# Layer 0's values, gates and reciprocal sums kept in DRAM by block of 128 tokens

## The chip, the cores and the metric

The kernel runs on one core of a Trainium2 chip. The metric is the device time of one execution, in microseconds (us). A core has five engines that work side by side: TensorE (PE; matmuls, its weight loads are listed as PEld), VectorE (DVE), ScalarE (ACT), GpSimd (POOL) and SyncE (SP). SP computes nothing: it issues DMA transfers from an in-order queue, and when one transfer has to wait, all behind it in that queue wait too.

## The reference, cut to what matters

A two-layer decoder on x of 2048 tokens by 1024 features, all in float32. Layer 0 runs two attentions of 8 heads each over one input projection, multiplies their joined output by a SiLU gate, projects it, and adds and normalises. Layer 1 (sliding window) does the same with other heads and is not touched by the change.

```
h = x @ w_in
cq, ckv, k_pe, fq, fk, fv, f_logit, gate = _split(h, EVEN_SIZES)
...
o_mla = causal_block_attention(q_mla, k_mla, v_mla, (MLA_NOPE + MLA_ROPE) ** -0.5)
...
o_fox = causal_block_attention(_heads(fq, FOX_HEADS), _heads(fk, FOX_HEADS),
                               _heads(fv, FOX_HEADS), FOX_DIM ** -0.5, cum)
o = jnp.concatenate([_merge(o_mla), _merge(o_fox)], axis=-1)
return (o * jax.nn.silu(gate)) @ w_out
```

and then `x = layer_norm(ALPHA * x + y, g, b)`.

## The kernel before

Five phases follow each other. Phase 1 (to about 595 us of the span) projects x; among its results are the SiLU gates, which `feature_tile` stores to the DRAM tensor `g1`, 32 stores of 256 KB. Phase 2 (to about 1522 us) runs the 16 heads of layer 0, each in four chunks `c` of 512 query tokens. `produce` makes the unnormalised probabilities of one chunk and stores the reciprocals of their row sums to `rd`; `consume` turns them and multiplies by the values, and stores the unnormalised output to `og1[c]` (64 stores of 128 KB). The two run interleaved: while one chunk is produced, the one before it is consumed. Phase 3 is the output projection of layer 0: 16 blocks `t` of 128 tokens. `load_og` loads a block's gates (`load_gate`, tile gt), the reciprocal sums (two loads, each spread over 64 partitions, tile rb) and values (tile og), multiplies them on POOL and DVE, and splits the product into a high part `oh` (ACT) and a low part `ol` (DVE); `out_block` then runs 48 matmuls of 128x512 (eight weight tiles, three products each, two halves), adds x, takes the statistics, and every second block normalises two blocks and stores them to `x1` (`finish`). Phases 4 and 5 are layer 1.

What sets the order around the change: a scheduler arranges the instructions of each engine, and each engine then runs its list in order. Nearly all loads of phases 2 and 3 share SP's queue. In phase 3 the gates and sums of a block are loaded into the buffers that later hold its `oh` and `ol` (three of each), so they wait until an earlier block's matmuls have freed them. The values have one buffer:

```
og = opool.tile([128, KB, 128], F32, name="og", bufs=1)
```

so the values of the next block are issued only when `ol` of the block before has been made from it. The rows z of x have five buffers, and a z load waits for the store of a block five earlier. Two blocks are prepared ahead by `prefetch`, which runs during the last chunk of the last head: it loads output weights, the gates and values of tokens 0 to 255, and multiplies them on POOL.

Of the kernel before, what the change touches and what calls it, by code (L numbers as in the profile page):

```python
# [9 lines left out]
F32 = mybir.dt.float32  # L10
# [29 lines left out]
def decoder_trunk(ctx, tc, x, x_t, w_lat, w_main, w_u, g_lat, b_f, w_out1, ln1,  # L40
# [20 lines left out]
    rd = dram.tile([16, T], F32, name="rd")  # L61
    g1 = dram.tile([D, T], F32, name="g1")
    og1 = [dram.tile([128, KB, 512], F32, name=f"og1_{c}") for c in range(4)]
# [122 lines left out]
    def phase1(late):  # L186
# [145 lines left out]
        def feature_tile(n, m, chunk, xT, w):  # L332
# [14 lines left out]
            else:  # L347
# [4 lines left out]
                queue.dma_start(out=g1[p * 128:(p + 1) * 128, tcs], in_=sg[:])  # L352
# [124 lines left out]
    def load_gate(gt, rb, t0, n):  # L477

        nc.sync.dma_start(out=gt, in_=g1[:, t0:t0 + n].rearrange("(k p) t -> p k t", p=128))
        for s_ in range(2):  # L480
            nc.sync.dma_start(out=rb[s_ * 64:s_ * 64 + 64], in_=rd[:].rearrange("(k s) t -> s k t", s=2)[s_:s_ + 1, :, t0:t0 + n].broadcast_to([64, KB, n]))

    def phase2(ctx, kpool):
# [25 lines left out]
        def produce(n, c, st):  # L509
# [55 lines left out]
            nc.sync.dma_start(out=rd[h if mla else 8 + h, tcs].rearrange("(j p) -> p j", p=128), in_=rec[:])  # L565

        def consume(n, c, P):
# [18 lines left out]
            def finish(po):  # L586
# [4 lines left out]
                queue.dma_start(out=og1[c][(hd % 2) * 64:(hd % 2) * 64 + 64, hd // 2, :], in_=t2[:])  # L591
# [45 lines left out]

        def prefetch():
# [9 lines left out]
            gts, rbs = (ppool.tile([128, T], F32, name="p")[:].rearrange("p (k q) -> p k q", k=KB) for _ in range(2))  # L648
            load_gate(gts, rbs, 0, 256)
            for t in range(2):  # L650
                nc.sync.dma_start(out=wout["og"][t], in_=og1[0][:, :, tok(t)])
            nc.gpsimd.tensor_tensor(out=gts, in0=gts, in1=rbs, op=OP.mult)
            for t in range(2):
                nc.gpsimd.tensor_tensor(out=wout["og"][t], in0=wout["og"][t], in1=gts[:, :, tok(t)], op=OP.mult)
            for steps, k, tag in ((PRE[0], 7, "vv"), (PRE[1], 4, "ka"), (PRE[2], 6, "kb")):
                for _ in range(steps):
                    yield 1
                wo_split(k, tag, raw[k], True)
            for _ in range(99):
                yield 1  # L660
# [6 lines left out]
        for n, c in todo + [(None, None)]:  # L667
            st = []
            gens = []
            if (n, c) == (15, 3):  # L670
                r3, r5 = wo_load(kpool.tile([128, T], F32, name="cb"), 3, 5)
            if n is None:
# [105 lines left out]
    def phase3(stack4, kpool, wout):  # L778
        with ExitStack() as ctx:
# [14 lines left out]
            def load_og(t):  # L794
                hl = parts()
                gt, rb = (bits(v[:]) for v in hl)
                load_gate(gt, rb, t * 128, 128)
                og = opool.tile([128, KB, 128], F32, name="og", bufs=1)
                nc.sync.dma_start(out=og[:], in_=og1[t // 4][:, :, tok(t % 4)])
# [462 lines left out]
```

## Time and profile before

| | us |
|---|---|
| median of 3 runs | 2666.89 (2655.42 to 2667.24) |
| the profiled execution, its own time | 2674.29 |
| its span, first to last instruction | 2672.5 |
| PE busy in the span | 2471.1 (92%) |
| mean granted TensorE clock | 0.962 |
| moved by DMA | 360.91 MB, 135 GB/s over the span |

The span is what the profile's rows are timed in; 1.8 us of the execution lie outside it. The profiled execution was 7.4 us slower than the median of the runs, so a saving read from its rows is taken off the median.

### The profile page before, as it was taken

The numbers are of one execution on the slowest core, as the hardware profiler recorded it, in microseconds if no ns is written. First come the engines' busy times: TensorE is split into PE (matmuls) and PEld (weight loads), VectorE is DVE, ScalarE is ACT, GpSimd is POOL, SyncE is SP. The second block draws the span as 40 slices with busy tenths as digits, with TensorE's granted clock in tenths as the row PEclk, the third lists the DMA queues.
The fourth block names the chain that finished last, engine by engine and source line by source line (L and its number), as shares of the span: only waits on it lengthen the run. The fifth ranks groups of instructions, "written<-read, shape, count | busy, mean of one in ns | idle before, by whom it ended". The sixth has DMA issues, their size and how long they took to land.

```text
span 2672.5 us, 36349 instructions
## 1 busy us (share of the span) xinstructions
PE 2471.1 (92%) x12885; PEld 2050.3 (77%) x12885; DVE 1531.1 (57%) x3002; ACT 1172.7 (44%) x2409; POOL 707.0 (26%) x694
## 2 busy tenths in 40 slices
PE   8999999999999999999999787659999999999997
PEld 7898888987788887888877665437888887777775
DVE  5442264317787877777777643345633644777775
ACT  3121222217676866777676501011121115566663
POOL 2010011101222221222222333232321321356555
PEclk9999999999999999999999888879999999999998
DMA  6574346654556665454554558854444653566563
GB/s 204 177 251 143 106 152 235 202 167 62 95 93 93 83 114 86 83 111 79 97 84 83 115 151 170 151 129 156 142 138 141 177 154 100 150 150 165 155 155 103
DMA packets 298566, 360.91 MB, mean 135 GB/s; under 512 B 55920, under 2 KB 202352, under 8 KB 293776
## 3 DMA queue, kind: packets, MB, share of 16 engines
q1 hardware_dynamic: 294224, 343.51, 53.6%
q0 software_dynamic: 4160, 15.08, 1.5%
q8 instruction: 102, 1.67, 0.3%
q14 instruction: 80, 0.66, 0.2%
HBM read 240.20 MB, written 118.29 MB: 134 GB/s over the span
## 4 chain that ended last, share of the span: by engine, by line
PE 68%; DMA 17%; DVE 5%; POOL 3%; ACT 3%; issue 3%; SPq 1%; POOLq 0%; DVEq 0%; ACTq 0%
PE pm L91 11%; PE pm L89 11%; PE pm L90 10%; PE pt L604 6%; DMA og<-og 5%; PE S L547 4%; PE S L548 4%; PE po L581 3%; PE po L582 3%; DMA kb<-kf 3%; DMA q<-qr 3%; DMA q<-qf 2%; PE S L1061 2%; PE py L727 2%; PE S L550 2%
## 5 line engine op out<-in xcount | busy, mean ns | idle before, releaser
L76 DVE TENSOR_TENSOR tl<-pt,th 128x512 fp32r<-128x512 f32 (+3 forms) x672 | 400.7, 611 | 128.4 <-ACT th L75 125.2
L89 PE MATMUL pm<-xh,w 128*128 128x512 f32 x1088 | 428.7, 394 | 7.5 <-DVE z L734 5.6
L75 ACT CAST th<-pt 128x512 fp32r<-128x512 f32 (+3 forms) x672 | 340.4, 524 | 203.2 <-PE pt L604 168.1
L91 PE MATMUL pm<-xh,w 128*128 128x512 f32 x1088 | 425.9, 392 | 0.0
L90 PE MATMUL pm<-xl,w 128*128 128x512 f32 x1088 | 425.6, 391 | 0.0
L604 PE MATMUL pt<-ident,p 128*128 128x128 f32 x2176 | 348.0, 280 | 4.0 <-DVE tl L76 3.9
L561 ACT ACTIVATE p<-p,mx 128x128 f32<-128x128 f32 (+15 forms) x256 | 309.0, 1207 | 29.3 <-DVE mx L558 27.5
L604 PEld LDWEIGHTS pt<-ident,p 128*128 128x128 f32 x2176 | 271.8, 145 | 58.6 <-DVE tl L76 7.3
L547 PE MATMUL S<-ka,q 96*128 96x512 f32 (+5 forms) x640 | 253.4, 396 | 29.6 <-DMA q<-qf 11.5
L581 PE MATMUL po<-th,vv 128*128 128x512 f32 (+2 forms) x640 | 278.0, 434 | 0.6 <-DVE t L589 0.4
L82 POOL TENSOR_SCALAR w<-w_raw 128x1024 fp32r<-128x1024 f32 (+3 forms) x88 | 98.5, 1132 | 581.3 <-PE pm L91 418.8
L89 PEld LDWEIGHTS pm<-xh,w 128*128 128x128 f32 x1088 | 205.0, 188 | 49.5 <-issue 7.3
L582 PE MATMUL po<-tl,vv 128*128 128x512 f32 (+2 forms) x640 | 238.3, 373 | 0.0
L91 PEld LDWEIGHTS pm<-xh,w 128*128 128x128 f32 x1088 | 204.7, 188 | 42.9
L90 PEld LDWEIGHTS pm<-xl,w 128*128 128x128 f32 x1088 | 204.9, 188 | 41.6
L609 POOL TENSOR_SCALAR th<-tf 128x512 fp32r<-128x512 f32 x96 | 59.4, 618 | 668.8 <-ACT tf L608 363.8
L548 PE MATMUL S<-kb,q 96*128 96x512 f32 (+5 forms) x640 | 234.4, 369 | 0.0
L83 DVE TENSOR_TENSOR w<-w_raw,w 128x1024 fp32r<-128x1024 f32 (+3 forms) x89 | 138.6, 1572 | 130.4 <-POOL w L82 127.4
L558 DVE CUSTOM_DVE_ANT_0 p<-S,zm 128x1024 f32<-128x1024 f32 (+7 forms) x128 | 123.7, 967 | 104.4 <-PE S L550 103.4
L547 PEld LDWEIGHTS S<-ka,q 128*128 128x128 f32 (+1 forms) x640 | 124.5, 194 | 54.5 <-issue 23.3
L1062 DVE CUSTOM_DVE_ANT_0 p<-S,bm,nsk 128x256 f32<-128x256 f32 x256 | 117.7, 477 | 71.8 <-PE S L1061 69.7
L1064 ACT ACTIVATE p<-p,mx 128x256 f32<-128x256 f32 x256 | 129.0, 505 | 66.2 <-DVE mx L1062 65.7
(249 smaller groups left out, 4771.0 us busy)
## 6 DMA issues: line engine op xcount, KB each, us to landing
w_raw<-in_w_main_dram SPq DMA_DIRECT2D x40, 512.0 KB, 5.2
w_raw<-in_w_odd_dram SPq DMA_DIRECT2D x36, 512.0 KB, 4.5
vd<-s_v SPq DMA_DIRECT2D x64, 256.0 KB, 2.7
vv<-vd SPq DMA_DIRECT2D x16, 1024.0 KB, 10.6
qs<-hl SPq DMA_DIRECT2D x64, 256.0 KB, 3.5
qt<-qs SPq DMA_DIRECT2D x64, 256.0 KB, 5.3
ka<-kf SPq DMA_DIRECT2D x16, 512.0 KB, 9.4
kb<-kf SPq DMA_DIRECT2D x16, 512.0 KB, 9.0
```

The source lines that it names most:

```text
L75: nc.scalar.copy(out=hi, in_=src)
L76: nc.vector.tensor_tensor(out=lo, in0=src, in1=bits(hi), op=OP.subtract)
L83: nc.vector.tensor_tensor(out=lo, in0=src, in1=bits(hi), op=OP.subtract)
L89: nc.tensor.matmul(ps, lhsT=ah, rhs=bh, start=(i == 0), stop=False)
L90: nc.tensor.matmul(ps, lhsT=ah, rhs=bl, start=False, stop=False)
L91: nc.tensor.matmul(ps, lhsT=al, rhs=bh, start=False, stop=(i == n - 1))
L547: nc.tensor.matmul(dst, lhsT=q0[ds, js], rhs=ka[ds, ks_], start=True, stop=False)
L548: nc.tensor.matmul(dst, lhsT=q0[ds, js], rhs=kb_[ds, ks_], start=False, stop=not (mla or diag))
L561: nc.scalar.activation(out=p[:, 0:L], in_=p[:, 0:L], func=AF.Exp, scale=-1.0, bias=acc[:], accum_out=su[:, j:j + 1])
L581: nc.tensor.matmul(po[0][:, q_:512], lhsT=vv[:, kb, :], rhs=th[:, k, q_:512], start=(kb == 0), stop=False)
L582: nc.tensor.matmul(po[0][:, q_:512], lhsT=vv[:, kb, :], rhs=tl[:, k, q_:512], start=False, stop=(kb == c * 4 + 3))
L604: nc.tensor.transpose(out=pt[:, k, :], in_=P[j][:, kk:kk + 128], identity=ident[:])
```

## The change

Three DRAM tensors get another layout. The gates `g1` were feature by token, so that one block of 128 tokens was read in pieces of 128 floats (512 bytes), eight per partition; now a block's eight pieces lie behind each other and one partition's row is 4 KB. The values `og1` and the reciprocal sums `rd` are laid out in the same way. In return, the stores to `g1` and `og1` are cut into four pieces of 512 bytes per partition where they were one of 2 KB. The stores to `rd` are of single floats in both kernels.

The gates and sums of block 0 get tiles of their own (`early0`, `early1`), whose loads are written at the start of the last chunk (15, 3). The gates and sums of block 1 are loaded in `prefetch` into the two halves of one buffer, where tokens 0 to 255 were loaded together into two buffers. The products for blocks 0 and 1 move from POOL (gate times sum for both blocks in one instruction, then values times that, two instructions) to DVE (values times gate, then times sum, four instructions), and stand behind the splits of the weights 7, 4 and 6.

```
-    rd = dram.tile([16, T], F32, name="rd")
-    g1 = dram.tile([D, T], F32, name="g1")
-    og1 = [dram.tile([128, KB, 512], F32, name=f"og1_{c}") for c in range(4)]
+    rd = dram.tile([NB, 2, KB, 128], F32, name="rd")
+    g1 = dram.tile([NB, 128, KB, 128], F32, name="g1")
+    og1 = [dram.tile([4, 128, KB, 128], F32, name=f"og1_{c}") for c in range(4)]
...
-                queue.dma_start(out=g1[p * 128:(p + 1) * 128, tcs], in_=sg[:])
+                queue.dma_start(out=g1[chunk * 4:chunk * 4 + 4, :, p, :].rearrange("j p t -> p j t"), in_=sg[:].rearrange("p (j t) -> p j t", j=4))
...
-    def load_gate(gt, rb, t0, n):
+    def load_gate(gt, rb, t):
-        nc.sync.dma_start(out=gt, in_=g1[:, t0:t0 + n].rearrange("(k p) t -> p k t", p=128))
+        nc.sync.dma_start(out=gt, in_=g1[t])
         for s_ in range(2):
-            nc.sync.dma_start(out=rb[s_ * 64:s_ * 64 + 64], in_=rd[:].rearrange("(k s) t -> s k t", s=2)[s_:s_ + 1, :, t0:t0 + n].broadcast_to([64, KB, n]))
+            nc.sync.dma_start(out=rb[s_ * 64:s_ * 64 + 64], in_=rd[t, s_:s_ + 1].broadcast_to([64, KB, 128]))
...
-            nc.sync.dma_start(out=rd[h if mla else 8 + h, tcs].rearrange("(j p) -> p j", p=128), in_=rec[:])
+            hd = h if mla else 8 + h
+            nc.sync.dma_start(out=rd[c * 4:c * 4 + 4, hd % 2, hd // 2, :].rearrange("j p -> p j"), in_=rec[:])
...
-                queue.dma_start(out=og1[c][(hd % 2) * 64:(hd % 2) * 64 + 64, hd // 2, :], in_=t2[:])
+                queue.dma_start(out=og1[c][:, (hd % 2) * 64:(hd % 2) * 64 + 64, hd // 2, :].rearrange("j p t -> p j t"), in_=t2[:].rearrange("p (j t) -> p j t", j=4))
...
-            load_gate(gts, rbs, 0, 256)
+            gates = [early, [v.rearrange("p (k q) -> p k q", q=128) for v in halves(ppool.tile([128, T], F32, name="p")[:])]]
+            load_gate(*gates[1], 1)
...
-            nc.gpsimd.tensor_tensor(out=gts, in0=gts, in1=rbs, op=OP.mult)
-            for t in range(2):
-                nc.gpsimd.tensor_tensor(out=wout["og"][t], in0=wout["og"][t], in1=gts[:, :, tok(t)], op=OP.mult)
...
+            for t in range(2):
+                for v in gates[t]:
+                    tc.keep_in_program_order(nc.vector.tensor_tensor(out=wout["og"][t], in0=wout["og"][t], in1=v, op=OP.mult))
...
+                early = [pool.tile([128, KB, 128], F32, name=f"early{i}")[:] for i in range(2)]
+                load_gate(*early, 0)
...
-                load_gate(gt, rb, t * 128, 128)
+                load_gate(gt, rb, t)
...
-                nc.sync.dma_start(out=og[:], in_=og1[t // 4][:, :, tok(t % 4)])
+                nc.sync.dma_start(out=og[:], in_=og1[t // 4][t % 4])
```

On DVE, at the end of phase 2 (L76/`tl` are the splits of turned probabilities for the last head, `cb` holds the values of blocks 0 and 1, `p` the gates and sums of block 1), there stood before:

```order
L83 TENSOR_TENSOR kb<-p,kb 128x1024
L76 TENSOR_TENSOR tl<-pt,th 128x4x128
L589 TENSOR_TENSOR t_15244<-po,t_15244 64x512
L76 TENSOR_TENSOR tl<-pt,th 128x4x128 x3
L76 TENSOR_TENSOR tl<-pt,th 128x128
L76 TENSOR_TENSOR tl<-pt,th 128x2x128
```

and now:

```order
L83 TENSOR_TENSOR kb<-p,kb 128x1024
L76 TENSOR_TENSOR tl<-pt,th 128x4x128
L590 TENSOR_TENSOR t_15249<-po,t_15249 64x512
L76 TENSOR_TENSOR tl<-pt,th 128x4x128 x2
L662 TENSOR_TENSOR cb<-cb,early_14934 128x1024
L76 TENSOR_TENSOR tl<-pt,th 128x4x128
L662 TENSOR_TENSOR cb<-cb,early_14935 128x1024
L662 TENSOR_TENSOR cb<-cb,p 128x1024
L76 TENSOR_TENSOR tl<-pt,th 128x128
L662 TENSOR_TENSOR cb<-cb,p 128x1024
L76 TENSOR_TENSOR tl<-pt,th 128x2x128
```

So four products stand among the last five splits that PE's last matmuls of phase 2 wait for. On POOL, at the same place, there stood before:

```order
L598 MEMSET tl 128x128
L652 TENSOR_TENSOR p<-p 128x2048
L654 TENSOR_TENSOR cb<-cb,p 128x1024 x2
L82 TENSOR_SCALAR oh<-cb 128x1024 x2
L591 DMA og_3_89<-t_15339 64x512
```

and now (L82 is the split into the high parts of blocks 0 and 1):

```order
L599 MEMSET tl 128x128
L82 TENSOR_SCALAR oh<-cb 128x1024 x2
L592 DMA og_3_89<-t_15344 64x4x128
L82 TENSOR_SCALAR wo_hi_15401<-cb 128x1024
L806 TENSOR_TENSOR og<-og,oh 128x1024 x2
```

So POOL's three products are gone from in front of the split. On SP's queue the early loads were moved far ahead of where they are written: the gates into the start of phase 2, and the sums behind the stores of the reciprocals that they read. The later one of these, in the last head, now stands so:

```order
L592 DMA og_2_88<-t_14611 64x4x128
L566 DMA rd<-rec 128x4x1
L481 DMA early_14935<-rd 64x1024
L527 DMA q_14939<-qf_77 64x512
L528 DMA q_14939<-qf_78 64x512
L566 DMA rd<-rec 128x4x1
```

There the load of the sums stands directly behind the store it reads, and ahead of the queries of the last chunk. The order of phase 3 on PE, DVE, ACT and SP is unchanged, apart from the shapes.

## Rows read from the trace of the kernel before

**Rows 1.** The page: the chain that ended last, shares by engine.

```profile
PE 68%; DMA 17%; DVE 5%; POOL 3%; ACT 3%; issue 3%; SPq 1%; POOLq 0%; DVEq 0%; ACTq 0%
```

**Rows 2.** Busy time by stretch, us and count; clock, DMA share, GB/s.

```profile
1540.00:1820.00 280.00, 192.82 (x730) 148.69 (x730) 112.02 (x120) 33.47 (x34) 87.22 (x67) 0.84 0.70 154
```

**Rows 3.** The chain of phase 3, 1546.6 to 1823.8: shares; first wait.

```profile
by line: DMA og<-og 52.9%; POOL og L800 11.1%; DVE og L801 5.8%; POOL z L772 4.7%; issue 4.6%; DMA x<-z 4.0%; POOL z L771 3.4%; DVE ol L83 2.9%; ACT oh L80 2.3%; ACT z L768 1.8%; DVE st L735 1.8%; DVE z L734 1.8%; POOL lr L108 1.0%; POOL x 
...
1546.60 15.66 DMA og<-og
```

**Rows 4.** The same chain over one pair of blocks: start, us, what.

```profile
1718.39 18.17 DMA og<-og
...
1736.69 2.34 POOL og L800
...
1739.06 1.23 DVE og L801
...
1752.51 2.42 POOL og L800
...
1758.67 18.67 DMA og<-og
```

**Rows 5.** SP's queue ahead of that load: start, us, issue.

```profile
1714.60 0.33 SPq L721 DMA_DIRECT2D z<-in_x_dram  x1
1715.03 0.39 SPq L479 DMA_DIRECT2D oh<-g  x1
1715.50 1.87 SPq L481 DMA_DIRECT2D ol<-rd  x2
1718.39 2.41 SPq L799 DMA_DIRECT2D og<-og  x1
```

**Rows 6.** Stretches of DMA work, columns as in Rows 2.

```profile
1498.50:1502.00 3.50, 3.50 (x23) 2.80 (x21) 2.29 (x7) 3.50 (x6) 0.00 (x0) 1.00 0.98 382
1502.50:1509.00 6.50, 4.01 (x29) 3.50 (x28) 5.87 (x7) 5.44 (x9) 3.17 (x4) 0.94 1.07 49
1721.50:1730.50 9.00, 7.63 (x34) 6.01 (x32) 0.00 (x0) 0.00 (x0) 0.00 (x0) 1.00 0.96 41
1731.50:1735.00 3.50, 0.00 (x0) 0.00 (x0) 0.00 (x0) 0.00 (x0) 0.00 (x0) 0.79 1.03 254
2262.50:2265.00 2.50, 2.50 (x13) 2.07 (x12) 0.47 (x1) 1.65 (x2) 0.00 (x0) 1.00 1.07 246
```

**Rows 7.** The page's DMA issues: count, KB each, us to landing.

```profile
w_raw<-in_w_odd_dram SPq DMA_DIRECT2D x36, 512.0 KB, 4.5
...
z<-in_x_dram SPq DMA_DIRECT2D x16, 512.0 KB, 5.3
...
rd<-rec SPq DMA_DIRECT2D x64, 2.0 KB, 11.3
```

**Rows 8.** Timeline of PE, and the chain, from phase 2 into phase 3.

```profile
1503.45 25.32 DMA p<-rd
...
1521.85 0.28 PE L582 MATMUL po<-tl,vv 128*128 128x256 f32 x1
1539.20 0.80 PE L727 MATMUL py<-ka,oh 128*128 128x512 f32 x1 [17.06 <-POOL oh L82]
```

**Rows 9.** Timeline of DVE at the end of phase 2.

```profile
1511.82 1.27 DVE L76 TENSOR_TENSOR tl<-pt,th 128x512 fp32r<-128x512 f32 x2
1516.20 1.46 DVE L76 TENSOR_TENSOR tl<-pt,th 128x512 fp32r<-128x512 f32 x3 [3.12 <-ACT th L75]
```

**Rows 10.** Timeline of PE: first and last matmul of block 15.

```profile
1824.83 0.39 PE L727 MATMUL py<-ka,oh 128*128 128x512 f32 x1
...
1835.48 0.40 PE L729 MATMUL py<-wo_hi,ol 128*128 128x512 f32 x1
```

**Rows 11.** SP's queue in the last head.

```profile
1461.05 0.38 SPq L565 DMA_DIRECT2D rd<-rec  x1
...
1469.38 0.45 SPq L527 DMA_DIRECT2D q<-qf  x1
```

More of the change, by code (lines that the diff above doesn't have):

```diff
@@ L636, in wo_split, with halves @@
             wout[k] = (v[:, 0:D], v[:, D:T])
+        def halves(t):
+            return t[:, 0:D], t[:, D:T]
         def prefetch():
@@ L647, in prefetch @@
             wout["og"] = [ogs[:, t * D:(t + 1) * D].rearrange("p (k q) -> p k q", q=128) for t in range(2)]
-            gts, rbs = (ppool.tile([128, T], F32, name="p")[:].rearrange("p (k q) -> p k q", k=KB) for _ in range(2))
-            load_gate(gts, rbs, 0, 256)
+            gates = [early, [v.rearrange("p (k q) -> p k q", q=128) for v in halves(ppool.tile([128, T], F32, name="p")[:])]]
+            load_gate(*gates[1], 1)
             for t in range(2):
-                nc.sync.dma_start(out=wout["og"][t], in_=og1[0][:, :, tok(t)])
-            nc.gpsimd.tensor_tensor(out=gts, in0=gts, in1=rbs, op=OP.mult)
-            for t in range(2):
-                nc.gpsimd.tensor_tensor(out=wout["og"][t], in0=wout["og"][t], in1=gts[:, :, tok(t)], op=OP.mult)
+                nc.sync.dma_start(out=wout["og"][t], in_=og1[0][t])
             for steps, k, tag in ((PRE[0], 7, "vv"), (PRE[1], 4, "ka"), (PRE[2], 6, "kb")):
```

## The prediction, made before the changed kernel was run

> **What bounds the kernel now.** I read the page's chain first. PE holds 68% of it and DMA 17% [rows 1], so the question is in which stage the DMA share lies. The table of stretches shows a hole in PE only in phase 3: in 1540 to 1820 us PE works 192.82 of 280 us at a granted clock of 0.84, while the DMA engines are 0.70 busy at a mean of no more than 154 GB/s [rows 2]. The chain of that stretch then names the wait: of 277.2 us, loads of og hold 52.9% (146.6 us, ten waits, the first 15.66) and one wait for the store to x1 4.0% (11.1 us); POOL's and DVE's products with og, 11.1% and 5.8%, follow [rows 3]. So PE does not bound phase 3. A loop of one buffer does: values land, POOL multiplies, DVE multiplies, ACT and DVE split, and only then the next values are issued.
>
> One pair of blocks shows the loop. From one issue of og to the one two blocks later it takes 1758.67 - 1718.39 = 40.28 us, of which the load is 18.17; the other 22.1 us are work in program order, among it POOL's normalising, which ends before 1752.51 and hides the load of the second block [rows 4]. Why 18 us for 512 KB? The queue ahead of it tells: z, the gates and two loads of sums are issued in the 4 us before, so four times 512 KB (2.1 MB) have to pass [rows 5]. The rates of stretches, matched with the queue's order, tell which of them is slow. While the sums pass, the DMA engines are 0.96 busy and move 41 GB/s; while the values pass, in the same pieces of 512 bytes, 254 GB/s; a stretch of output weights in rows of 4 KB ran at 382 GB/s [rows 6]. The sums are one row read for 64 partitions, in pieces of 512 bytes. At 41 GB/s their 0.52 MB would take 12.8 us; the bulk of the 18 us is theirs.
>
> **Loads of phase 3.** Each of the loads of gates, sums and values gets rows of 4 KB, so an eighth of the pieces. For gates and values the price is bounded by 254 GB/s (nothing gained) and 382 GB/s. For sums in rows of 4 KB there is no row here. The slow end is 41 GB/s, if reading one place 64 times is what costs; the quick end 382. The nearest row is in phase 5, where four loads of the other layer's sums, each one row of 2 KB read for 64 partitions, set the pace at 246 GB/s [rows 6]. That is the same kind of load with pieces four times as long, so I take the quick side.
>
> Then 2.1 MB at 382 GB/s take 5.5 us, and as the queue's first transfer is issued 3.8 us ahead of the values [rows 5], little is left but the delay of one load. Loads of 512 KB in rows of 4 KB land in 4.5 us (weights) and 5.3 us (z), in the median [rows 7]. I take 5.0 for each of the nine later og waits, and for the wait for the x1 store, which shares the engines with the same loads. For the first, which has two more 512 KB in front, 7. The eleven waits come from 146.6 + 11.1 = 157.7 us to 10 x 5.0 + 7 = 57: **101 us saved**. The bounds: 3.7 us each (5.5 + 2 - 3.8, where 2 is my estimate for a landing behind its data, from 4.5 less a passage of about 1.4, with a second load often in front) would give 114; 10 us each, as if only half of the wait were due to the pieces, 48.
>
> By the Trainium skill, page "DMA: Bandwidth & Descriptors", section "Specifications", a transfer of 512 bytes or more runs at line rate, so longer rows would save nothing. The trace does not bear it out for this load, at 41 against 382 GB/s [rows 6]. By the rule alone the term of 101 us would be 0.
>
> **Does PE then bound?** Block 15 ran without a gap: 1824.83 to 1835.48 + 0.40, 11.05 us for 48 matmuls [rows 10]. Sixteen blocks are 177 us. The loop of a pair becomes 22.1 + 5 = 27.1 us against PE's 22.1, so in the later blocks PE still waits some 2.5 us a block; the blocks 2 to 4 come about as quickly as PE takes them, and there I give back 2 us.
>
> **Start of phase 3.** PE ends phase 2 at 1522.1 and starts block 0 at 1539.20, after 17.06 us of waiting for POOL's split; what POOL waited for before it was 25.32 us of loading sums [rows 8]. Now POOL's three products are gone from in front of the split, and block 0 needs only values from the late loads, block 1 0.5 MB of gates, 0.5 of sums and 0.5 of values. But they cannot pass quickly: the DMA engines stand at 49 GB/s from 1502.5 to 1509 [rows 6], just behind the last store of reciprocals, which is made of single floats and which the change leaves as it is. From 1509 the rest of the weights, gates, sums and block 0's values are 2.1 MB, 5.5 us at 382 GB/s, so I have them at about 1515.5 with the delay of landing, and block 1's at 1517. DVE reaches the first product at 1511.82 + 1.27 = 1513.1 and, in order, holds up the splits behind it by 2.4 us; before, it stood idle for 3.12 us there [rows 9]. The four products at 1.23 us (the same shape, DVE's product with og [rows 4]) are 4.9 us. Of these 2.4 + 4.9 = 7.3 us the idle time takes 3.1 and gaps between the later splits some 1; I have the last split, and with it PE's end of phase 2, 3.3 us later, at 1525.4. POOL's split of block 0 is done by then, so PE starts block 0 at once: 1539.2 - 1525.4, **14 us saved**. Bounds: 17 us if nothing is held up; 7 us if the loads stay as slow as before (1528.8 at the landing, plus two products of 1.23, a split of about a microsecond). The same 14 us move the loads of block 2, which stand behind the splits of the last weights, so they count once for the whole loop.
>
> **What it costs.** The stores: 32 of 256 KB and 64 of 128 KB in pieces of 512 bytes. At 254 in place of 382 GB/s they take 0.34 and 0.17 us longer, 22 us of DMA time in all, in phases in which I find no wait on a store; I put 0 on the path, 22 at most. Early gates: 512 KB between queries in the first microseconds of phase 2, 1.4 us of passage at 382 GB/s; I count 1. Early sums: SP waits until the store in front has landed, 11.3 us in the median [rows 7]. In the last head the store is issued at 1461.05 and the queries behind it at 1469.38 [rows 11], so they come 3 us late; they are for a chunk that starts after the next two stores, over 10 us later, so nothing. If that cover were gone, 3 us.
>
> Sum: 101 + 14 - 2 - 1 = 112 us. The profiled execution's 2674.3 becomes 2562; the median of the runs is 7.4 lower, so 2666.9 - 112 = **2555**.
>
> **Rivals.**
> *PE becomes the bound.* If all waits fall to 3.7 us or less, phase 3 is 177 us of PE from about 1524 on, ending at 1701 where it ended at 1835.9: 135 saved, 2532. For it: PE needs 22.1 of the 27.1 us. Against it: the 22.1 us of ordered work in the loop do not get shorter. 1 in 10.
> *The loads gain by half.* The og waits stay near 10 us, for the rows are longer but z, x1 stores and layer 1's weights share the engines: 48 + 14 - 3 = 59 saved, 2608; between it and the forecast lies all that is partial. 15 in 100.
> *The sums stay slow.* Reading one row 64 times costs what it costs: 12.8 us per block stay, and only gates and values gain, 2 x 0.7 us a block, some 25 us with what the rest of the queue gives, and 10 at the start: 35 saved, 2632. Against it the 246 GB/s of phase 5. 5 in 100.
> *Row length does nothing.* The slow stretch has another cause, as contention with z and stores; only the start gains: 2653. This is what the rule would do here (Trainium skill, "DMA: Bandwidth & Descriptors", "Specifications"). 2 in 100.
> *Slower.* The stores in pieces behave as the reciprocals' store does, 49 GB/s: 128 KB in 2.7 us, 256 KB in 5.3 us, 342 us in all for 96 stores, with queries and keys queued behind them. Half of it on the path makes 2667 - 112 + 171 = 2726; a third undoes the gain. Against it: pieces of 512 bytes were loaded at 254 GB/s. 3 in 100.
>
> **How the numbers follow.** The forecast has the remaining 65 in 100, by itself 2540 to 2575 (waits of 4 to 7 us). The runs of one kernel spread by 0.4%, so 0.5% (13 us) is about what counts as a difference: faster is the forecast and the first three rivals, 0.95; the same is the rule, 0.02; slower 0.03. For 8 in 10 I take the forecast, PE as the bound, and the nearer part of the partial gain: 2532 to 2592.
>
> **What would show it.** In phase 3: no stretch of high DMA share below 100 GB/s; og waits on the chain of 4 to 7 us; a pair in 26 to 29 us; PE busy above 80% of the stage and its clock above 0.84. At its start: PE's first matmul of block 0 within some 2 us of its last of phase 2, at about 1525, and DVE waiting for values at its first product. Phases 1 and 2 as long as before within 3 us. I am wrong if the sums' loads still show 40 GB/s, if POOL or DVE's ordered work grows when it is no longer spread out, or if the stores show up as waits of PE.

## The result, and the profile after

The changed kernel took 2925.09 us (median of 4 runs, 2907.36 to 2929.44) against 2666.0 for the kernel before: a ratio of 1.0966 with a 95% interval of 1.0939 to 1.0992. It is slower by a tenth, where 2555 us and a range of 2532 to 2592 were forecast. Its profiled execution has a span of 2923.9 us against 2672.5, and a mean granted clock of 0.926 against 0.962.

The page of the changed kernel: the chain by engine and by line (it answers to [rows 1]), and the GB/s of the 40 slices of the span.

```profile
PE 59%; DMA 25%; DVE 5%; ACT 3%; POOL 3%; issue 3%; another core or an unknown queue 2%; SPq 1%; DVEq 0%; POOLq 0%; ACTq 0%
PE pm L89 10%; PE pm L91 10%; PE pm L90 10%; DMA q<-qr 8%; DMA q<-qf 5%; PE pt L605 4%; DMA kb<-kf 4%; DMA og<-t 3%; PE S L547 2%; PE S L548 2%; PE po L582 2%; PE S L1067 2%; PE py L733 2%; PE py L734 2%; PE py L735 2%
...
GB/s 196 200 228 101 131 198 221 201 49 45 80 64 78 68 81 58 69 77 60 83 44 82 55 78 37 177 241 183 173 135 149 135 164 118 148 156 156 169 157 94
```

The DMA share of the chain rose from 17% to 25%, and its DMA lines are no longer loads of og but loads of queries and keys (q, kb) and stores of values (og<-t): phase 2. From the ninth slice on, 585 to 1827 us, the DMA engines move 37 to 83 GB/s.

The table of stretches of the kernel before, phase 2 and phase 3 (columns as in [rows 2]: stretch and length, then busy us of PE, PEld, DVE, ACT and POOL with counts, granted clock, DMA share, GB/s):

```profile
595.00:1522.10 927.10, 879.93 (x5198) 737.73 (x5197) 696.21 (x1444) 662.77 (x1222) 206.30 (x323) 0.97 0.55 90
1539.20:1835.90 296.70, 209.52 (x802) 162.52 (x803) 123.26 (x130) 38.17 (x38) 96.21 (x75) 0.85 0.66 146
```

and of the changed kernel, the same phases, then two short stretches inside phase 2, then two of phase 3:

```profile
595.00:1865.30 1270.30, 952.89 (x5199) 789.23 (x5197) 703.07 (x1448) 663.82 (x1222) 206.91 (x323) 0.85 0.60 67
1866.40:2095.10 228.70, 191.10 (x802) 150.98 (x803) 130.31 (x145) 38.92 (x40) 96.71 (x75) 0.93 0.62 200
...
613.00:623.00 10.00, 0.00 (x0) 0.00 (x0) 1.12 (x2) 0.77 (x2) 0.00 (x0) 0.67 0.97 20
...
642.00:656.00 14.00, 1.08 (x7) 0.57 (x5) 2.24 (x6) 2.75 (x4) 0.00 (x0) 0.68 0.91 13
...
1999.60:2001.00 1.40, 1.31 (x3) 1.12 (x4) 1.36 (x4) 0.00 (x0) 0.00 (x0) 0.50 1.03 421
2001.00:2003.00 2.00, 2.00 (x7) 1.57 (x7) 0.74 (x2) 0.00 (x0) 0.00 (x0) 0.70 1.07 348
```

Phase 3 came out shorter, by 296.7 - 228.7 = 68.0 us, and the hole in front of it, PE's idle time between the phases, shrank from 1539.2 - 1522.1 = 17.1 to 1.1 us. In the two short stretches of it that are shown, its loads of sums, gates, z and values pass at 421 and 348 GB/s, where the sums stood at 41 [rows 6]. All of that was forecast in kind, with 99 us for phase 3. But phase 2 takes 1270.3 us in place of 927.1, 343 more, with the same 5198 matmuls. 73 us of it are PE's busy time (952.9 against 879.9, at a mean granted clock of 0.85 against 0.97, where 1.00 is the upper of its two levels, 2.4 GHz), the other 270 idle time. In the two short stretches inside phase 2 the DMA engines are 0.97 and 0.91 busy and move 20 and 13 GB/s, and PE does next to nothing. 343 - 68 - 16 leaves 259; the rest of the span is 8 us shorter: 251.

What the stretches wait for is in the chain of phase 2 of the changed kernel (595 to 1865; shares by line, then the longest pieces: start, us, what):

```profile
by line: DMA q<-qr 18.5%; DMA q<-qf 10.7%; PE pt L605 10.1%; DMA kb<-kf 9.3%; DMA og<-t 7.5%; PE S L547 5.6%; PE S L548 5.1%; PE po L582 5.1%; PE po L583 4.6%; another core or an unknown queue 4.1%; PE S L550 3.6%; issue 2.9%; DMA rd<-rec 2
...
633.85 22.64 DMA q<-qr
874.78 21.00 DMA og<-t
1182.79 21.80 DMA og<-t
1295.90 20.95 DMA q<-qf
1328.55 26.81 DMA og<-t
1486.38 26.27 DMA og<-t
1767.24 25.19 DMA rd<-rec
```

Four of these seven pieces are waits for stores of values (og<-t), which the change cut into pieces of 512 bytes. The chain alone can't tell whether these are slow themselves or are held up by another store; e1 and e2 below ask it. In SP's queue, at the first and the last of the seven (start, us, issue):

```profile
606.60 0.38 SPq L566 DMA_DIRECT2D rd<-rec  x1
...
613.14 15.17 SPq L525 DMA_DIRECT2D q<-qr  x2
...
632.88 0.38 SPq L566 DMA_DIRECT2D rd<-rec  x1
633.30 0.96 SPq L525 DMA_DIRECT2D q<-qr  x2
...
656.14 0.31 SPq L525 DMA_DIRECT2D q<-qr  x1
...
1767.24 0.38 SPq L566 DMA_DIRECT2D rd<-rec  x1
1792.45 0.45 SPq L481 DMA_DIRECT2D early<-rd  x1
```

Both of these stretches follow a store of reciprocals (rd<-rec). The one issued at 632.88 has a small load of queries (32 KB) behind it, issued in the same microsecond, which is 22.64 us under way. The one issued at 1767.24 keeps a load of sums waiting for 25.19 us. Before, such a store landed after 11.3 us in the median [rows 7]. So PE waits for queries (the waits of PE in phase 2; line, what ended the wait, us in all, times, longest):

```profile
PE S L547 <- DMA q<-qf: 76.6, 8, 16.3
PE S L550 <- DMA q<-qr: 75.4, 15, 13.5
PE po L582 <- DVE t L590: 49.3, 8, 11.6
PE S L547 <- DMA q<-qr: 39.6, 6, 9.1
```

In the third line PE waits for DVE to empty `po`, which stands behind the stores of values. Before, no wait of PE for queries in phase 2 was longer than 3.9 us.

### The profile page after: what moved, and what is told of

The parts are those of the page before. It is cut to its first block, busy times and chain, and to the rows that moved or that the text cites. A ratio compares the mean times of both kernels' runs of the same rounds, so it can differ in the third digit from the quotient of the medians.

```text
span 2923.9 us, 36360 instructions
## 1 busy us (share of the span) xinstructions
PE 2522.6 (86%) x12885; PEld 2088.5 (71%) x12885; DVE 1539.7 (53%) x3006; ACT 1174.1 (40%) x2409; POOL 698.5 (24%) x691
## 4 chain that ended last, share of the span: by engine, by line
PE 59%; DMA 25%; DVE 5%; ACT 3%; POOL 3%; issue 3%; another core or an unknown queue 2%; SPq 1%; DVEq 0%; POOLq 0%; ACTq 0%
PE pm L89 10%; PE pm L91 10%; PE pm L90 10%; DMA q<-qr 8%; DMA q<-qf 5%; PE pt L605 4%; DMA kb<-kf 4%; DMA og<-t 3%; PE S L547 2%; PE S L548 2%; PE po L582 2%; PE S L1067 2%; PE py L733 2%; PE py L734 2%; PE py L735 2%
## 5 line engine op out<-in xcount | busy, mean ns | idle before, releaser
L76 DVE TENSOR_TENSOR tl<-pt,th 128x512 fp32r<-128x512 f32 (+3 forms) x672 | 402.1, 611 | 186.4 <-ACT th L75 180.0
L547 PE MATMUL S<-ka,q 96*128 96x512 f32 (+5 forms) x640 | 271.5, 424 | 156.1 <-DMA q<-qf 76.6
L605 PE MATMUL pt<-ident,p 128*128 128x128 f32 x2176 | 366.2, 290 | 35.6 <-DVE tl L76 26.4
L605 PEld LDWEIGHTS pt<-ident,p 128*128 128x128 f32 x2176 | 286.6, 151 | 96.9 <-DVE tl L76 27.7
L582 PE MATMUL po<-th,vv 128*128 128x512 f32 (+2 forms) x640 | 289.0, 452 | 49.6 <-DVE t L590 49.3
L547 PEld LDWEIGHTS S<-ka,q 128*128 128x128 f32 (+1 forms) x640 | 135.7, 212 | 185.1 <-issue 149.5
L548 PE MATMUL S<-kb,q 96*128 96x512 f32 (+5 forms) x640 | 249.9, 393 | 0.0
L583 PE MATMUL po<-tl,vv 128*128 128x512 f32 (+2 forms) x640 | 247.0, 386 | 0.7 <-DVE tl L76 0.7
L82 POOL TENSOR_SCALAR w<-w_raw 128x1024 fp32r<-128x1024 f32 (+3 forms) x88 | 97.8, 1125 | 589.1 <-PE pm L91 417.8
L83 DVE TENSOR_TENSOR w<-w_raw,w 128x1024 fp32r<-128x1024 f32 (+3 forms) x89 | 139.4, 1581 | 130.1 <-POOL w L82 127.2
L550 PE MATMUL S<-ka,q 96*128 96x512 f32 (+2 forms) x320 | 130.1, 408 | 75.4 <-DMA q<-qr 75.4
L558 DVE CUSTOM_DVE_ANT_0 p<-S,cb 128x1024 f32<-128x1024 f32 (+7 forms) x128 | 123.1, 967 | 109.9 <-PE S L548 96.2
```

Of the source, the lines that this page charges most:

```text
L76: nc.vector.tensor_tensor(out=lo, in0=src, in1=bits(hi), op=OP.subtract)
L547: nc.tensor.matmul(dst, lhsT=q0[ds, js], rhs=ka[ds, ks_], start=True, stop=False)
L548: nc.tensor.matmul(dst, lhsT=q0[ds, js], rhs=kb_[ds, ks_], start=False, stop=not (mla or diag))
L558: nc.vector.tensor_tensor_reduce(out=p[:, s0:s0 + w], in0=S[:, b:b + w], in1=in1, op0=OP.add, op1=OP.min, scale=-scale, scalar=3e38 if acc ...
L582: nc.tensor.matmul(po[0][:, q_:512], lhsT=vv[:, kb, :], rhs=th[:, k, q_:512], start=(kb == 0), stop=False)
L583: nc.tensor.matmul(po[0][:, q_:512], lhsT=vv[:, kb, :], rhs=tl[:, k, q_:512], start=False, stop=(kb == c * 4 + 3))
```

## The theory and its rivals

**Theory A.** The store of reciprocals became slow. It is of 512 single floats in both kernels, but they go to four places (one for each block of a chunk): before, these lay side by side, 512 bytes apart; the new layout puts them 8 KB apart. While such a store is under way it holds up what else is in the DMA engines and in SP's queue. Rivals: **B**, the stores of values and gates in pieces of 512 bytes are what is slow (the prediction's last rival); **C**, the early loads hold up the queue, since a load of sums waits for the store in front of it.

## The experiments

All lines are of the changed kernel, and edits are to it, where nothing else is said. "Phase 2" below is from 595 us to the last product with values (po, L583 in the changed kernel), "phase 3" from the first matmul with ka to the last with vv, by the first and last starts that the trace gives for these tiles; by that measure the kernel before has 927 and 295, the changed one 1270 and 227. Each experiment but e12 is one execution. The kernel before took 2649.7, 2642.6, 2640.1 and 2641.4 us on the chips of the four sets of runs, so times are compared within a set. Its phases are known from the first runs alone (those of the result above), in an execution of 2674.3 us, 25 to 34 us more than beside the experiments; so a difference of that size between a phase of an experiment and one of the kernel before can be the set's, and some of one against the changed kernel too.

| run | us | before beside it | phase 2 | phase 3 |
|---|---|---|---|---|
| e1 sums old | 2637.2 | 2649.7 | 923.5 | 280.2 |
| e2 values and gates old | 2875.7 | 2649.7 | 1210.2 | 236.2 |
| e3 sums stored as rows | 2537.4 | 2649.7 | 883.6 | 225.4 |
| e4 places 8.5 KB apart | 2596.4 | 2649.7 | 940.5 | 226.5 |
| e5 places 4 KB apart | 2667.3 | 2642.6 | 1012.7 | 224.7 |
| e6 places 16 KB apart | 2864.8 | 2642.6 | 1209.4 | 226.2 |
| e7 four stores, 8 KB apart | 3312.2 | 2642.6 | 1656.3 | 227.1 |
| e9 places 9 KB apart | 2570.2 | 2640.1 | 914.4 | 226.6 |
| e10 four stores, 8.5 KB apart | 2603.9 | 2640.1 | 949.6 | 225.6 |
| e11 rows, no early loads | 2535.1 | 2640.1 | 879.1 | 226.2 |
| e12 rows, timed | 2536.7 | 2640.1 | 882.3 | 224.9 |
| e13 before, sums as rows | 2610.2 | 2641.4 | 874.4 | 294.9 |
| e14 rows, values and gates old | 2547.2 | 2641.4 | 883.7 | 234.1 |

### Which part is it: e1, e2

e1, the sums' layout undone:

```
-    rd = dram.tile([NB, 2, KB, 128], F32, name="rd")
+    rd = dram.tile([16, T], F32, name="rd")
...
-            nc.sync.dma_start(out=rd[c * 4:c * 4 + 4, hd % 2, hd // 2, :].rearrange("j p -> p j"), in_=rec[:])
+            nc.sync.dma_start(out=rd[hd, tcs].rearrange("(j p) -> p j", p=128), in_=rec[:])
...
-            nc.sync.dma_start(out=rb[s_ * 64:s_ * 64 + 64], in_=rd[t, s_:s_ + 1].broadcast_to([64, KB, 128]))
+            nc.sync.dma_start(out=rb[s_ * 64:s_ * 64 + 64], in_=rd[:].rearrange("(k s) t -> s k t", s=2)[s_:s_ + 1, :, tok(t)].broadcast_to([64, KB, 128]))
```

> The changed kernel with the reciprocal sums alone laid out as before (16 rows of 2048; a head's four blocks lie side by side, 2 KB for one store of single floats; read again in pieces of 512 bytes); values, gates and early loads as changed. Theory A (the stores of reciprocals got slow: 512 floats scattered over four places 8 KB apart take 18 to 25 us in place of 11 to 12, and the queue's later loads wait behind them): phase 2, 1271 us in the changed kernel and 927 before, comes back to 925 to 945; phase 3 keeps only part of its gain, since the sums are read in short pieces again, so 2924 - 335 + 20 to 80 = 2610 to 2670. Rival B (the stores of values in pieces of 512 bytes are slow, as the prediction's last rival had it): phase 2 stays near 1270 and the time is 2920 or more. Rival C (the early loads hold up the queue): phase 2 stays above 1200.

2637.2 us, phase 2 923.5. Phase 2 is as short as before (1.5 us below the range of A) although values and gates are stored in pieces: B and C fall as the cause of the 343 us. A remainder of some 20 us can't be ruled out: phase 3, the hole and the rest of the span are 34 us shorter than in the trace of the kernel before, but e1 as a whole is only 12.5 us faster than that kernel beside it. No run here assigns it.

e2, the other half undone: `g1`, `og1` and their stores and loads as before the change.

```
-    og1 = [dram.tile([4, 128, KB, 128], F32, name=f"og1_{c}") for c in range(4)]
+    og1 = [dram.tile([128, KB, 512], F32, name=f"og1_{c}") for c in range(4)]
```

> The changed kernel with values and gates laid out as before (stores in rows of 2 KB, loads of 128 tokens in pieces of 512 bytes); the sums by block and the early loads as changed. Theory A (stores of reciprocals): phase 2 stays at 1240 to 1290 us, the time 2910 to 2960. Rival B (stores of values and gates in pieces of 512 bytes): phase 2 comes back to 925 to 960 and the time to about 2590.

2875.7 us, phase 2 1210.2: still slow, as A has it, but 60 us shorter than in the changed kernel and so outside A's range by 30. Whether these 60 are the price of the pieces was open until e6 and e14.

### Taking the slow store away: e3

PE turns the four sums of a chunk into rows, and the store has four runs of 512 bytes:

```
-            nc.vector.reciprocal(out=rec[:], in_=su[:])
-            hd = h if mla else 8 + h
-            nc.sync.dma_start(out=rd[c * 4:c * 4 + 4, hd % 2, hd // 2, :].rearrange("j p -> p j"), in_=rec[:])
+            st.append(su)
...
+            def store_sums():
+                pr = ps_t.tile([128, 4, 128], F32, name="pt")
+                nc.tensor.transpose(out=pr[0:4, 0, :], in_=P[4][:], identity=ident[:])
+                rec = sm.tile([4, 128], F32, name="rec", bufs=2)
+                nc.vector.reciprocal(out=rec[:], in_=pr[0:4, 0, :])
+                nc.sync.dma_start(out=rd[c * 4:c * 4 + 4, hd % 2, hd // 2, :], in_=rec[:])
```

> The changed kernel, same layouts in DRAM, but the four sums of a head's chunk are first transposed on PE (128x4 to 4x128, one of the PSUM tiles of the transposes), DVE takes the reciprocal from there, and the store writes four rows of 512 bytes in place of 512 single floats; it is issued with the values' half of the work, one step later than now. Theory A: the 64 slow stores are gone altogether, phase 2 falls to 927 or below (880 to 927, PE alone was 880 busy before), phase 3 stays at 223: 2924 - 344 to 390 = 2530 to 2580. Rival B: phase 2 stays near 1270, 2920.

2537.4 us. Its stretches (columns as above) and the longest waits of PE from 595 to 1480:

```profile
595.00:1479.00 884.00, 869.38 (x5257) 724.87 (x5255) 735.26 (x1448) 669.02 (x1223) 209.25 (x324) 0.99 0.37 96
1479.00:1707.50 228.50, 191.40 (x805) 151.84 (x806) 131.01 (x146) 39.94 (x41) 97.92 (x77) 0.93 0.64 202
```

```profile
PE S L546 <- DVE mx L557: 4.6, 10, 0.5
PE pt L611 <- ACT tf L615: 2.8, 8, 0.7
PE S L549 <- DMA q<-qr: 2.8, 1, 2.8
```

Phase 2 is 386 us shorter than in the changed kernel with the same layouts in DRAM, and 43 shorter than in the trace of the kernel before, part of which is the set's (e13 has 31 us in all, within one set). The DMA engines are 0.37 busy for 96 GB/s, where 0.55 went with 90 before and 0.60 with 67 after: the single floats took engine time that moved next to nothing. PE works 869 of 884 us and waits 2.8 us for queries. The price is small: 64 transposes, and a reciprocal of 945 ns (4x128) on DVE in place of 173 (128x4), which nothing waits long for.

### Why is it slow: the distance of the places, e4, e5, e6, e9

The same place in the program shows one store by itself. Of the two early loads of sums, the first waits in SP's queue for one certain store (head 13, chunk 0), so the time from the issue of that store to the issue of the load is taken as the store's, and the same five loads of queries stand between in all of these kernels. e4 adds 512 bytes behind each block's 8 KB of sums, e9 adds 1 KB:

```
-    rd = dram.tile([NB, 2, KB, 128], F32, name="rd")
+    rd = dram.tile([NB, 2 * D + 128], F32, name="rd")
```

(2 * D + 256 in e9), with store and loads addressed accordingly. e5 puts even and odd heads into two tensors, so that blocks lie 4 KB apart, and e6 makes the tensor twice as large, so that they lie 16 KB apart:

```
+    rd = [dram.tile([NB, KB, 128], F32, name=f"rd{s}") for s in range(2)]
```

```
+    rd = dram.tile([NB, 4, KB, 128], F32, name="rd")
```

> The changed kernel with 512 bytes of padding behind each block's 8 KB of sums, so that the four places of one store lie 8.5 KB apart and not 8 KB; the rest as changed. Theory A1 (the store is slow because its places lie a power of two apart): phase 2 falls to 925 to 1000, time 2580 to 2650. Theory A2 (it is slow because the places are apart at all, or because of the order of the floats): phase 2 stays at 1240 to 1290, 2900 to 2940. Rival B: 2920 too.

> The changed kernel with the sums of even and odd heads in two tensors of their own, so that the four places of one store lie 4 KB apart and not 8 KB; loads are the same rows of 4 KB. Theory A1 (what costs is a distance that is a power of two, and more of it the larger it is) puts it between the 512 bytes of before (phase 2 of 927 us) and the 8 KB (1270): 1000 to 1250, time 2650 to 2900. Rival A3 (only the exact distance of 8 KB or more falls together): phase 2 at 925 to 960, time 2580 to 2610. Rival A4 (any distance of a power of two from a KB on is the same): 1250 to 1290, time 2900 to 2940.

> The changed kernel with the blocks' sums 16 KB apart in place of 8 KB (the other 8 KB of each stay unused); the rest as changed. Theory A1: as slow or slower, phase 2 at 1270 to 1700 us, time 2920 to 3350. Rival A2 (it is the places' being apart, of whatever distance): as at 8 KB, 2900 to 2940. If the distance of 8 KB were special by itself, phase 2 would fall towards 940.

> The changed kernel with 1 KB of padding behind each block's sums (places of one store 9 KB apart). The one store of sums that a load behind it waits for took 18.2 us at 8 KB, 19.0 at 16 KB, 12.2 at 4 KB, 9.8 at 8.5 KB and 9.0 with the places side by side. Theory A1 in its sharper form (single floats that fall on the same part of the memory are written one after another, and which part it is changes every 512 bytes or every KB): the four places fall on four different parts, that store takes 5 to 10 us, phase 2 900 to 945 us, time 2560 to 2600. If only the odd half KB matters: back to 15 us or more, 2750 or above.

SP's queue, the store and the load that waits for it. The changed kernel (8 KB):

```profile
1614.30 0.37 SPq L566 DMA_DIRECT2D rd<-rec  x1
...
1632.48 0.45 SPq L481 DMA_DIRECT2D early<-rd  x1
```

e1 (512 bytes, side by side):

```profile
1326.33 0.37 SPq L566 DMA_DIRECT2D rd<-rec  x1
...
1335.36 0.61 SPq L481 DMA_DIRECT2D early<-rd  x1
```

e4 (8.5 KB):

```profile
1356.14 0.37 SPq L567 DMA_DIRECT2D rd<-rec  x1
...
1365.96 0.45 SPq L481 DMA_DIRECT2D early<-rd  x1
```

e5 (4 KB):

```profile
1414.66 0.37 SPq L566 DMA_DIRECT2D rd<-rec  x1
...
1426.89 0.45 SPq L481 DMA_DIRECT2D early<-rd  x1
```

e6 (16 KB):

```profile
1565.15 0.37 SPq L566 DMA_DIRECT2D rd<-rec  x1
...
1584.10 0.45 SPq L481 DMA_DIRECT2D early<-rd  x1
```

e9 (9 KB):

```profile
1331.77 0.37 SPq L567 DMA_DIRECT2D rd<-rec  x1
...
1341.43 0.45 SPq L481 DMA_DIRECT2D early<-rd  x1
```

So one store takes 9.0 us side by side, 12.2 at 4 KB, 18.2 at 8 KB and 19.0 at 16 KB, but 9.8 at 8.5 KB and 9.7 at 9 KB. The second early load, which stands directly behind the store it waits for, gives the same picture: 10.0, 15.0, 25.2 and 23.9 us, but 10.0 and 9.5. With the sums as rows (e3) the first early load stands 2.5 us behind its store. Phase 2 goes the same way: 923.5, 1012.7, 1270.0, 1209.4, 940.5, 914.4. Being apart by 8.5 or 9 KB costs little or nothing; being apart by 8 KB or 16 KB costs twice the time, and half a KB of padding undoes it. Of what was expected, A1 held in e4 and e9; in e5 it held with its lower end (A1 had 1000 to 1250), and in e6 the store was as slow as at 8 KB but phase 2 60 us below A1's range. In its sharper form A1 allowed the store 5 to 10 us in e9; it stayed at 9.7, so that 1 KB spreads the floats better than half a KB is not seen in the store, though phase 2 is 26 us shorter (in another set, in which the kernel before took 9.5 us less).

### Neighbours or addresses: e7, e10

If neighbouring floats of a store jump from place to place, is it the jumping? e7 issues a store for each block, 128 floats into one run of 512 bytes; e10 does that with the padding of e4.

```
-            nc.sync.dma_start(out=rd[c * 4:c * 4 + 4, hd % 2, hd // 2, :].rearrange("j p -> p j"), in_=rec[:])
+            for j in range(4):
+                nc.sync.dma_start(out=rd[c * 4 + j, hd % 2, hd // 2, :].rearrange("(p o) -> p o", o=1), in_=rec[:, j:j + 1])
```

> The changed kernel, layouts as changed, with each store of a chunk's sums issued as four stores of one block, 128 single floats into one run of 512 bytes each, so that neighbouring floats of a store no longer jump by 8 KB; 192 more stores in the queue, 0.4 us each to issue. Theory A5 (what costs is that neighbouring floats jump from place to place): phase 2 falls to 930 to 1000 us, time 2590 to 2660. Rival A6 (what costs is the number of single floats that meet in lines a power of two apart, in whatever order, since the four stores are in flight together): phase 2 stays at 1200 or above, time 2850 or more, and more queue places are held.

> The four stores of one block each (3312 us at 8 KB) with the padding of 512 bytes (8.5 KB apart). If the four stores were slow for their addresses alone, since all fall on one part of the memory: phase 2, 1657 us at 8 KB, falls to 930 to 1000, time 2590 to 2660. If they were slow because each store's 128 floats lie side by side, so that neighbouring floats meet in one run of 512 bytes: phase 2 stays above 1500, time above 3150. Between the two, what remains is the price of four places in the queue where one was held.

3312.2 us at 8 KB, 2603.9 at 8.5 KB. The same instructions, the same number of stores, and 512 bytes in an address make 708 us. The last product of phase 2 in the view by tile of e7 (count; ns min/median/max; first and last start):

```profile
L584 PE MATMUL po<-tl,vv x640: 276/393/776, 642.4 to 2251.3; 128*128 128x512 f32 x160
```

and of e10:

```profile
L585 PE MATMUL po<-tl,vv x640: 277/393/792, 617.1 to 1544.6; 128*128 128x512 f32 x160
```

A5 falls, the jumping is not the cause: A6 holds, and e10 says that it is the address alone. That single stores of e7 are slow is not shown: its two early loads stand 14.4 and 11.8 us behind the first of the four stores in front of them, in e10 11.6 and 10.4. What is slow is read from phase 2, with all four under way. Four queue places where one was held cost little when the stores are quick (949.6 against 940.5 in e4) and much when they are slow (1656 against 1270).

### The other parts of the change: e8, e11, e13, e14

> The kernel that stores the sums as four rows of 512 bytes (2537.4 us in its run), with the gates and sums of block 0 loaded with the others at the end of phase 2 and not early. If the early loads bring something by themselves, block 0 starts later: four loads of 0.5 MB and two of values, 3 MB, would pass in about 8 us at 382 GB/s after about 1457, so the products still have them before phase 2 ends at 1479: 0 to 5 us slower, 2537 to 2543. If early loads cost in phase 2, it is faster by a few us.

e8 tells nothing of its question: the loads were written later, but the early loads of sums stand in the queue at the same times (1316.8 and 1425.2 us against 1316.9 and 1425.3 in e3), and 2537.2 us only repeats e3. e11 takes the tiles away with the loads:

```
-                early = [pool.tile([128, KB, 128], F32, name=f"early{i}")[:] for i in range(2)]
-                load_gate(*early, 0)
...
-            gates = [early, [v.rearrange("p (k q) -> p k q", q=128) for v in halves(ppool.tile([128, T], F32, name="p")[:])]]
-            load_gate(*gates[1], 1)
+            gates = [[v.rearrange("p (k q) -> p k q", q=128) for v in halves(ppool.tile([128, T], F32, name="p")[:])] for t in range(2)]
+            for t in range(2):
+                load_gate(*gates[t], t)
```

> The kernel that stores the sums as rows of 512 bytes (2537.4 us in its run), with gates and sums of block 0 loaded at the end of phase 2 into a tile of the exponentials, as before the change, and no early loads in the program (in the run e8 the loads had stood in the queue where they were). In that kernel the two early loads of sums waited for nothing of note. If early loads bring something: block 0 starts 3 to 12 us later, 2540 to 2550. If not: 2534 to 2540.

2535.1 us beside 2536.7 in the same set: the early loads bring nothing once the others are quick.

e13 is the kernel before with nothing but the transposed sums and the store as rows (side by side, as its layout has them), the edit of e3 with `rd[hd, tcs].rearrange("(j p) -> j p", p=128)` as the place.

> The kernel before, its layouts untouched, with the sums alone transposed on PE and stored as rows of 512 bytes (side by side, 2 KB in all) in place of 512 single floats. Theory A says that the single floats cost time in the kernel before too, 9 to 12 us for each of 64 stores, most of it hidden: phase 2 falls from 927 to the 884 us of the kernel with rows and block layouts, phase 3 stays at 297 or, its loads being the slow ones, a little less: 2667 - 43 = 2610 to 2630 on the chip of the first run, or 30 to 45 below the kernel before beside it. If the 42 us came from the block layouts, it is within 10 us of the kernel before.

2610.2 us beside 2641.4: 31 less, phase 2 874.4, the hole behind it 9.4 in place of 17.3, phase 3 294.9 as before. Of the expected 30 to 45 it is the low end. Phase 2 alone seems to fall by 52 us, more than the whole gain; the 927 are those of the slower first runs. The single floats cost the kernel before as well.

e14 is e3 with values and gates laid out as in e2.

> The changed kernel with the sums stored as rows by block, and values and gates laid out as before (rows of 2 KB stored, pieces of 512 bytes loaded). If the stores of values in pieces of 512 bytes cost phase 2 something by themselves, phase 2 falls below the 884 us of the kernel with rows and block layouts (to 820 to 870, but PE alone needs 880, so it can't be much); if not, it stays at 880 to 890, and phase 3, 227 there, grows by 10 as it did between the changed kernel and e2: 2537 + 10 = 2540 to 2552. By the prediction's price for gates and values (0.7 us a load of 0.5 MB) it would be 2550 to 2560.

2547.2 us beside 2641.4; phase 2 883.7 as with values by block (883.6), phase 3 234.1 against 225.4, about the 10 us more that were expected. The stores in pieces cost nothing that can be seen; the loads of values and gates in long rows bring 9 us. The 60 us by which e2 was quicker than the changed kernel showed in e6 too, with the values in pieces. So they need no change of the pieces; what they follow from was not tried. A part may be the set's: the changed kernel itself ran only in the first runs, in which the kernel before took 16 and 23 us more than beside e2 and e6.

### The version that beats both: e12

> The kernel that stores the sums as four rows of 512 bytes, timed against the kernel before. From its single runs (2537.4 beside 2649.7 before): 0.955 to 0.960 of the time before if the difference holds, an interval that stays below 0.965. By the prediction's own account of phase 3 and the start (112 us) the ratio would be 0.958, but then phase 2 would have to be as long as before; it was 42 us shorter in the single run, and phase 3 28 us longer than forecast.

2536.69 us (2535.78 to 2538.15) against 2640.14: a ratio of 0.9609, interval 0.9591 to 0.9627, just above the 0.955 to 0.960 expected. The change's layouts with the sums stored as rows are 4% quicker than the kernel before.

## Why the prediction was wrong, point by point

**The step that failed** stands in the part on the start of phase 3: the store of reciprocals, "which is made of single floats and which the change leaves as it is". It did not: the edit to that line moved the four places of each store from 512 bytes to 8 KB apart. The prediction costed the stores of values and gates and gave none to this one. e1, e4 and e10 against e7 show in its place: 18.2 and 25.2 us for a store in place of 9.0 and 10.0, and 343 us of phase 2, 270 as idle time of PE and 73 as longer matmuls at the lower clock. "Phases 1 and 2 as long as before within 3 us" was named as what would show it, and phase 1 was.

**Stores of values and gates in pieces, 0 on the path:** right (e1, e14). So the rival on the slow side, 2726 us, had a side that came true for another store than its own: pieces of 512 bytes are quick, single floats are not. Its price for a bad store, 49 GB/s, was read right behind a store of single floats, and the one step not taken was to ask what sets that rate.

**Early sums, 0, or 3 us if the cover were gone:** the cover was the 10 us and more to the next use. With stores of 18 and 25 us it was gone, and the second early load alone held up SP's queue until 1792.45, 25.19 us on the chain. With quick stores it is 0 (e11).

**Loads of phase 3, 101 us:** the mechanism was right and the size of the waits too. The chain of phase 3 in the changed kernel, 1866.4 to 2095.1 (it answers to [rows 3, 4]):

```profile
by line: DMA og<-og 16.0%; POOL og L806 12.6%; issue 8.0%; POOL z L778 7.1%; DVE og L807 6.6%; DMA ol<-rd 5.5%; PE py L734 5.4%; PE py L735 5.4%; POOL z L777 5.2%; PE py L733 5.2%; DVE ol L83 3.6%; DVE st L741 3.0%; ACT z L774 2.7%; POOL lr
...
1999.66 6.97 DMA og<-og
2028.82 8.29 DMA og<-og
```

Waits for values and sums are 16.0 + 5.5 = 21.5% of 228.7, 49 us, against 157.7: 109 saved where 101 were forecast. But the phase is only 68 us shorter, where 101 - 2 = 99 were forecast. Two things stand between. First, the last of the eleven waits before (18.26 us from 1799.35 on) lay beside the last 35 us of PE in the phase, in which PE works without a gap in both kernels (columns as in [rows 2], before and after):

```profile
1800.58:1835.90 35.32, 35.32 (x159) 29.33 (x160) 16.28 (x20) 8.23 (x10) 10.40 (x9) 0.93 0.35 107
2060.39:2095.10 34.71, 34.71 (x159) 28.84 (x160) 22.52 (x34) 8.43 (x11) 10.51 (x9) 0.95 0.42 149
```

To shorten that wait brings the phase nothing, and 13 of the 101 us were counted for it. Second, from the first issue of og to that of block 15 the chain took 252.8 us before (1546.6 to 1799.4) and 186.4 after (1872.8 to 2059.2). Its waits fell from 139.4 to 49.1 us, but the work between them grew from 113 to 137: 10 us more of it on POOL, 4 on DVE, and 5.5 on PE, which had none. The mis-sized term is what is given back: 2 us forecast, some 24 measured, of which PE as the bound of early blocks is only 5.5. It is the sign of being wrong that the prediction named itself, that the ordered work of POOL and DVE "grows when it is no longer spread out". The prediction even had the number for it: its pair of 27.1 us makes 176 of the 252.8 us, 77 saved, and not 101. A pair of blocks takes 2028.82 - 1999.66 = 29.2 us, 7.0 of it the load; the 22.2 that are left are the 22.1 of the prediction to a tenth, so it was 2 us of load a pair that made 29 of 27. With waits of 3.7 to 8.4 us on the chain it was neither the rival of half a gain (waits near 10) nor that of PE as the bound that took from the gain. Sums and values share the gain unequally: phase 3 loses 295 - 280 = 15 us with values and gates by block alone (e1), 59 with the sums alone (e2).

**The rule on 512 bytes** (the Trainium skill, "DMA: Bandwidth & Descriptors", "Specifications": line rate from 512 bytes on) would have left phase 3 as it was. Values and gates come near to it, 9 us for eight times longer rows (e14); the sums, one row read for 64 partitions, do not: 41 GB/s in pieces of 512 bytes, 348 and more in the stretches of phase 3 above, in which they pass together with the other loads.

**Start of phase 3, 14 us:** right, 16 by the hole; whether phase 2 itself ended 3.3 us later, as forecast, can't be seen beneath the 343. PE's timeline in the changed kernel, to be laid beside [rows 8]:

```profile
1865.05 0.28 PE L583 MATMUL po<-tl,vv 128*128 128x256 f32 x1
...
1866.40 0.50 PE L733 MATMUL py<-ka,oh 128*128 128x512 f32 x1 [1.08 <-POOL oh L82]
```

The forecast and the failed step together: 2666 - 112 + 343 = 2897. Phase 3 gave 99 - 68 = 31 us less than forecast, the start 2 more, the rest of the span 8 that were not forecast, and the 1 us for early gates lies within the 343: 2897 + 31 - 2 - 8 - 1 = 2917, which is 2666 plus the 251 of the spans. The median was 2925, since the traced execution of the kernel before lay 8 us above its median and that of the changed kernel only 1.

## What to carry to other kernels

When a layout in DRAM is changed for its readers, cost each of its writers by what one element run becomes and how far apart the runs of one store fall: a store of a mere 2 KB, in single floats 8 KB apart, held up a queue for 18 and 25 us here. Turn such data on the chip and store rows; where that can't be done, pad the distance (8.5 and 9 KB were quick here, 4, 8 and 16 KB were not). And when waits go from a loop, walk the chain again with them gone: what stood beneath them (here 24 us of ordered work, and PE's last 35 us beside the last load) is what the gain is short of.

## What was not expected of the hardware

512 single floats to four places took, at one place of the program, 18.2 us at distances of 8 KB and 19.0 at 16 KB, 12.2 at 4 KB, but 9.0 to 9.8 us at 512 bytes, 8.5 KB and 9 KB. That floats at multiples of 8 KB are written one after another and others side by side would fit these times, and e7 against e10; it is not shown, and neither is what in the memory makes it so.

The Trainium skill, "DMA: Bandwidth & Descriptors", "Latency and other measured facts", tells of copies whose rate falls at row pitches of large powers of two (its smallest pitch is 512 KiB, and the fall is plain from 2 MiB on), and that 4 KiB of padding restored the rate at a pitch of 4 MiB while 192 bytes did not. These runs agree in kind, at a far smaller pitch of 8 KB, for single floats, and with half a KB of padding.

A slow store is not slow alone: at 613 to 623 us the DMA engines were 0.97 busy with 20 GB/s, the traffic being loads of queries and of gates behind a store of 2 KB. And PE's clock fell with it: with the stops of phase 2 the granted clock was 0.85 in place of 0.97, and the same matmuls took 73 us more.
